# A two-layer hybrid encoder on one core: separate banks for value products, the usual weight unit last, bias lines in rounded precision, block copies in two steps, and one weight chunk of mixer B by seven products

## The chip, the cores and the metric

The kernel runs on one core of a Trainium2 chip. The time is the device time of one execution in microseconds (us), and what counts is the median of several runs; the profile is one further execution taken by the hardware profiler. Five engines work side by side: TensorE (PE in the profile; its weight loads are PEld), VectorE (DVE), ScalarE (ACT), GpSimd (POOL) and SyncE (SP, which here only issues DMAs). Each engine executes its own list of instructions strictly in order; between engines they wait on semaphores. Matmul results go to PSUM, which has eight banks of 128 partitions by 512 floats.

## The reference, cut to what matters

The input is 256 positions by 2048 features in float32. Two layers follow each other: mixer A (grouped-query attention) with a gated MLP, then mixer B (three head groups of dilated attention) with a second gated MLP, and a last RMS norm.

```python
def mixer_b(h, w_qkv, w_o, rel_bias):
    qkv = (h @ w_qkv).reshape(b, s, n_g, 3, hg, HEAD_DIM)      # 2048 -> 9216
    for g, (window, dil) in enumerate(B_GROUPS):               # (128,1),(512,4),(2048,16)
        o, lz = dilated_group(qkv[:, :, g, 0], qkv[:, :, g, 1], qkv[:, :, g, 2],
                              rel_bias[:, g * hg:(g + 1) * hg], window, dil)
    wts = jax.nn.softmax(jnp.stack(log_zs, axis=0), axis=0)
    y = jnp.concatenate([wts[g][..., None] * outs[g] for g in range(n_g)], axis=2)
    return y.reshape(b, s, B_WIDTH) @ w_o

def conv_ffn(h, w_up, conv_w, conv_b, w_down):
    u = depthwise_conv(h @ w_up, conv_w) + conv_b              # 2048 -> 11264, 3 taps over positions
    gate, val = jnp.split(u, 2, axis=-1)
    return (jax.nn.silu(gate) * val) @ w_down                  # 5632 -> 2048
```

## The kernel before

**Products.** All large products are of 256 positions (two halves `m`, 128 each) by weights that stream in from memory. A weight tile is 512 rows by 512 columns, called a chunk `kg` of an output block `n`; it is loaded in two raw buffers of 512 KB (`raw`, `NRAW = 6` of them). Precision near float32 is kept by splitting both operands into a rounded high part and the rest: ACT writes `wh` (L128), DVE writes `wl = raw - wh` (L129), and PE does three products, `xh*wh`, `xh*wl`, `xl*wh` (L153 to L155). One raw buffer makes twelve matmuls of 512 columns, here called a usual unit, or `c`. The split pairs `wh`/`wl` lie in a ring of `NHL = 3`; the down projection of the MLP adds a fourth. `split_raw` gives these instructions a priority 45 places ahead, so they stand early in their engines' lists. `feed` and `project` run over the chunks; accumulators are bank pairs 0/1 and 2/3 in turn (`new_acc`), banks 4 to 7 go round for everything else (`ps_tile`).

**Seven products.** In the down projection two of the chunks are done for two output blocks `n0`, `n1` together by Strassen's scheme with seven products in place of eight (`project_pair`, L215). The two weight blocks are cut into "11", "12", "21", "22"; DVE adds blocks in place (L242), each product `P` takes six matmuls, and sums of the inputs (`forms`) are made beforehand. Products 2, 3 and 4 go straight into C11, C12 and C21; products 1, 5, 6 and 7 have banks of their own (M1, M5, M6, M7) and are added to the result by `combine`. Usual units of the other chunks stand between the products (`weave`).

**Woven work.** Attention and activation work is written as generators; `step()` advances the oldest one after each unit, so its instructions stand between matmuls. `heads_T_dve` turns a key or query tile into head-major form: DVE transposes 32x32 blocks into a staging tile (L335), then sixteen block copies place them, twelve on ACT (L347) and four on POOL (L345), all in one step (`turned`, L351). The staging tile is one buffer (tag `vl` in mixer B). `late_transpose` does the same for the next stage's input; its last block goes by PE.

**Mixer B** (L917): for each half `hf` of the heads and each group `g`: key projection, query projection, then three value projections. `k_gen` and `s_gen` scale (L686), turn, form logits (L305, or L307 to L309), add bias, and take exponentials (L986). `v_gen` turns probabilities and multiplies by values; for `g == 0` the products of heads 0 and 1 share one bank, as do those of 2 and 3 (L1037).

**Bias lines** (L892) makes the position bias during the first MLP: a one-hot table times the bias table, six float32 matmuls (L908), written to memory and read back in skewed form.

## Time and profile before

| what | value |
|---|---|
| median of 3 runs | 2263.91 us (2262.77 to 2263.95) |
| the profiled execution | 2264.28 us, of which span 2262.5 us |
| matmuls | 10093 records, 2241.2 us busy |
| VectorE, ScalarE, GpSimd busy | 1671.3, 1535.6, 299.2 us |
| read from memory | 429.20 MB, 192 GB/s over the span |

The span is the time between the first and the last instruction of the profile; the rest of the execution's time lies around it. The page of the profile has the busy time of each engine, the chain of work that ended last, the costliest groups of instructions and the DMA issues. Further views are asked of the trace: which engine waited for which, the instructions in order of time (start, length, engine, line, output and inputs; idle time ahead of them and who ended it stand in brackets), groups of equal instructions in a stretch, and busy times by stretch. Matmuls overlap, so a record of 0.39 us does not mean that each takes that long on the engine: the distance between two starts does.

### The profile page before, as it was taken

The page shows a single profiled execution, that of the slowest core. Times are in us where ns is not written, and L with a number is a line of the kernel's source. Part 1 is how long each engine was busy: PE and PEld are TensorE (multiplying, and loading weights), DVE is VectorE, ACT ScalarE, POOL GpSimd, SP SyncE. Part 2 cuts the span into 40 slices and gives each one's busy share as a digit, 9 for nine tenths or more (in the row PEclk, how much of TensorE's full clock was granted, in tenths as well). Part 3 has the DMA queues.
Part 4 walks back from the last instruction along what each step waited for, and adds up shares of the span by engine and source line. Part 5 has one row for each costly group of instructions (what it writes and reads, how often), then busy time and mean ns, then how long its engine had stood idle before and what let it go on. Part 6 is the DMA issues. An engine that isn't in the chain of part 4 may idle for free.

```text
span 2262.5 us, 28925 instructions
## 1 busy us (share of the span) xinstructions
PE 2241.2 (99%) x10093; PEld 1853.5 (82%) x10093; DVE 1671.3 (74%) x2267; ACT 1535.6 (68%) x2400; POOL 299.2 (13%) x436
## 2 busy tenths in 40 slices
PE   9999999999999999999999999999999999999998
PEld 7788888888888888888878887888888888888886
DVE  6776678888878788856575557465888788688895
ACT  6665777777547777767775777565777754577763
POOL 2211102210001010121130103000101100001101
PEclk9999999999999999999999999999999999999999
DMA  8444667765665655666655564655665656556654
GB/s 297 158 149 149 191 198 217 227 198 192 207 203 187 199 190 188 204 223 203 190 173 180 177 194 160 186 195 188 197 191 192 204 188 212 188 193 193 226 191 136
DMA packets 126452, 437.43 MB, mean 193 GB/s; under 512 B 17265, under 2 KB 18033, under 8 KB 126305
## 3 DMA queue, kind: packets, MB, share of 16 engines
q1 hardware_dynamic: 119744, 425.64, 58.3%
q0 software_dynamic: 6128, 9.38, 1.7%
q8 instruction: 79, 1.29, 0.2%
q14 instruction: 69, 0.56, 0.1%
q10 hardware_dynamic: 432, 0.56, 0.1%
HBM read 429.20 MB, written 6.29 MB: 192 GB/s over the span
## 4 chain that ended last, share of the span: by engine, by line
PE 91%; DVE 3%; ACT 2%; issue 1%; DMA 1%; POOL 1%; SPq 0%; POOLq 0%; DVEq 0%; ACTq 0%
PE acc L154 25%; PE acc L155 25%; PE acc L153 25%; PE acc L273 5%; PE acc L275 5%; PE acc L278 5%; DVE wl L129 1%; ACT tM L347 1%; ACT wh L128 1%; PE ps L305 1%; PE ps L307 0%; PE ps L309 0%; POOL pp L345 0%; PE ps L308 0%; DMA raw<-in_w_down_dram 0%
## 5 line engine op out<-in xcount | busy, mean ns | idle before, releaser
L129 DVE TENSOR_TENSOR wl<-raw,wh 128x1024 fp32r<-128x1024 f32 x828 | 1019.0, 1237 | 437.8 <-ACT wh L128 435.2
L128 ACT ACTIVATE wh<-raw 128x1024 fp32r<-128x1024 f32 x828 | 872.6, 1058 | 499.9 <-PE acc L155 307.0
L153 PE MATMUL acc<-wh,xh 128*128 128x512 f32 x2176 | 851.2, 392 | 0.6 <-ACT wh L164 0.6
L154 PE MATMUL acc<-wl,xh 128*128 128x512 f32 x2176 | 848.2, 390 | 1.6 <-DVE wl L129 1.4
L155 PE MATMUL acc<-wh,xh 128*128 128x512 f32 x2176 | 847.7, 390 | 0.0
L154 PEld LDWEIGHTS acc<-wl,xh 128*128 128x128 f32 x2176 | 408.8, 188 | 88.6 <-DVE wl L129 4.4
L155 PEld LDWEIGHTS acc<-wh,xh 128*128 128x128 f32 x2176 | 408.6, 188 | 84.7
L153 PEld LDWEIGHTS acc<-wh,xh 128*128 128x128 f32 x2176 | 408.9, 188 | 84.0 <-ACT wh L164 1.0
L345 POOL COPY u<-t 32x256 f32<-32x256 f32 x176 | 110.6, 628 | 1027.1 <-DVE t L455 1018.9
L273 PE MATMUL acc<-wh,ah 128*128 128x512 f32 x520 | 202.5, 389 | 1.5 <-DVE h L408 1.5
L275 PE MATMUL acc<-wh,al 128*128 128x512 f32 x520 | 202.3, 389 | 0.0
L154 PE MATMUL acc<-wl,ah 128*128 128x512 f32 x480 | 187.1, 390 | 1.0 <-DVE wl L129 1.0
L153 PE MATMUL acc<-wh,ah 128*128 128x512 f32 x480 | 187.2, 390 | 0.3 <-DVE cu L628 0.3
L155 PE MATMUL acc<-wh,al 128*128 128x512 f32 x480 | 186.8, 390 | 0.0
L347 ACT ACTIVATE u<-t 32x256 f32<-32x256 f32 x352 | 147.7, 420 | 13.9 <-DVE t L455 6.0
L278 PE MATMUL acc<-wl,ah 128*128 128x512 f32 x520 | 146.1, 389 | 0.0
L273 PEld LDWEIGHTS acc<-wh,ah 128*128 128x128 f32 x520 | 97.6, 188 | 22.6 <-DVE h L408 2.3
L278 PEld LDWEIGHTS acc<-wl,ah 128*128 128x128 f32 x520 | 97.6, 188 | 20.3
L275 PEld LDWEIGHTS acc<-wh,al 128*128 128x128 f32 x520 | 97.6, 188 | 20.2
L154 PEld LDWEIGHTS acc<-wl,ah 128*128 128x128 f32 x480 | 90.2, 188 | 20.0 <-DVE wl L129 1.8
L153 PEld LDWEIGHTS acc<-wh,ah 128*128 128x128 f32 x480 | 90.1, 188 | 19.1 <-DVE cu L628 0.9
L155 PEld LDWEIGHTS acc<-wh,al 128*128 128x128 f32 x480 | 90.1, 188 | 18.6
(182 smaller groups left out, 1729.0 us busy)
## 6 DMA issues: line engine op xcount, KB each, us to landing
raw<-in_w_up_dram SPq DMA_DIRECT2D x352, 512.0 KB, 4.4
raw<-in_w_down_dram SPq DMA_DIRECT2D x176, 512.0 KB, 4.8
raw<-in_w_b_dram SPq DMA_DIRECT2D x144, 512.0 KB, 4.4
raw<-in_w_bo_dram SPq DMA_DIRECT2D x48, 512.0 KB, 3.9
raw<-in_w_a_dram SPq DMA_DIRECT2D x40, 512.0 KB, 4.5
raw<-in_w_ao_dram SPq DMA_DIRECT2D x32, 512.0 KB, 4.0
raw<-in_w_a_dram SPq DMA_DIRECT2D x16, 256.0 KB, 6.6
h<-in_x_dram SPq DMA_DIRECT2D x4, 512.0 KB, 8.4
```

Of the source, the lines that this page charges most:

```text
L128: nc.scalar.activation(wh, r, AF.Copy)
L129: nc.vector.tensor_tensor(wl, r, wh.bitcast(F32), ALU.subtract)
L153: nc.tensor.matmul(accs[m], xh, wh[:, j, :], start=st, stop=False)
L154: nc.tensor.matmul(accs[m], xh, wl[:, j, :], start=False, stop=False)
L155: nc.tensor.matmul(accs[m], xl, wh[:, j, :], start=False, stop=sp)
L273: nc.tensor.matmul(acc[k], xh, wh[:, j, :], start=k in fresh, stop=False)
L275: nc.tensor.matmul(acc[k], xl, wh[:, j, :], start=False, stop=False)
L278: nc.tensor.matmul(acc[k], xh, wl[:, j, :], start=False, stop=last[k] == i and j == 1)
L305: nc.tensor.matmul(o, lh[ls], rh[rs], start=start, stop=stop)
L345: nc.gpsimd.tensor_copy(dst, src)
L347: nc.scalar.activation(dst, src, AF.Copy)
```

## The change

Five things are changed.

1. In `v_gen` every product of group 0 takes its own bank.
2. In the first down pair of each MLP's first half, the first and the eighth product are no longer followed by a usual unit, so that two usual units move behind the last products; and `combine` takes M7 where it took M5 in its last sum, which is algebraically equal.
3. The bias table is split into a rounded high part and the rest, which stand in the two halves of the partitions, against a one-hot table that is loaded twice; the matmul is then one rounded product.
4. `turned` copies its sixteen blocks in two steps of eight, with one idle step fewer behind it.
5. In mixer B the key and query projections of groups 1 and 2, in both halves, are made together by `seven`: chunk 3 by seven products, chunks 0 to 2 by twelve usual units. The input forms are made once, at the end of the first MLP (`last_forms`). M1, M5, M6 and M7 take banks from the common four and are moved out at once (`product_done`).

```diff
+    def project_pair(w, n0, n1, lhs, forms, units, late, early_done, n0_done, product_done=None):
+        if product_done:
+            acc = dict(zip(("C11", "C21", "C12", "C22"), new_acc() + new_acc()))
...
+            for k, *_ in todo:
+                if k not in acc:
+                    acc[k] = ps_tile()
...
+            if product_done and kind == "P" and home[p][0] == "M":
+                product_done(home[p], acc.pop(home[p]))
             if i == last_s:
                 early_done(acc)
-            if i == last["C21"]:
+            if i == max(last["C11"], last["C21"]):
                 n0_done(acc)
-            step()
+            if not product_done or kind == "c" or p in (1, 5, 7, 4):
+                step()
...
     def turned(o, s, pool, tag):
         t = turn_blocks(s, pool, tag)
+        for part in (range(8), range(8, 16)):
+            yield
+            place_blocks(o.rearrange("p j (m t) -> p j m t", m=2), t, "paaa", part)
+
+    def last_forms(hT, turn_pair, n, g):
+        fm = hT["forms"] = {f: new_hT(4 * n + i)[:2] for i, f in enumerate((1, 0, 2, 4))}
...
+        c0 = scaled(0)
+        put(1, c0[:, :, :P])
+        put(0, c0[:, :, P:])
         yield
-        place_blocks(o.rearrange("p j (m t) -> p j m t", m=2), t, "paaa")
+        c1 = scaled(1)
+        put(2, c1[:, :, :P])
+        put(4, c1[:, :, P:])
+        x0, s1, s2, s3, s4 = (tmp(k) for k in (12, 13, 14, 15, 20))
+        yield
+        nc.scalar.activation(x0, c0[:, :, P:], AF.Copy)
+        nc.vector.tensor_tensor(s3, c0[:, :, :P], x0, ALU.subtract)
+        nc.vector.tensor_tensor(s1, c1[:, :, P:], x0, ALU.subtract)
+        put(7, s3)
+        put(5, s1)
+        yield
+        nc.vector.scalar_tensor_tensor(s2, s1, -1.0, c0[:, :, :P], ALU.mult, ALU.subtract)
+        nc.vector.tensor_tensor(s4, c1[:, :, :P], s2, ALU.add)
+        put(6, s2)
+        put(3, s4)
...
+                    lone = (ps[0], ps[7]) if lead > 1 and hf == 0 else ()
                     for u in ps:
-                        units += [u] + [c.pop(0) for _ in range(min(1, len(c)))]
+                        units += [u] + [c.pop(0) for _ in range(min(1, len(c))) if u not in lone]
...
-                    nc.vector.tensor_tensor(u, acc["M5"], u, ALU.add)
-                    nc.vector.tensor_tensor(hcol(1, n1), hcol(1, n1), u, ALU.subtract)
+                    nc.vector.tensor_tensor(v, acc["M7"], v, ALU.add)
+                    nc.vector.tensor_tensor(hcol(1, n1), hcol(1, n1), v, ALU.subtract)
...
-            oh = wp.tile([P, 1024], F32, tag="wh9", name="oh")
-            nc.gpsimd.dma_start(oh, onehot)
+            of = lp.tile([P, 2, 512], F32, tag="tT", name="of").rearrange("p a c -> p (a c)")
+            oh = wp.tile([P, 1024], F32R, tag="wh9", name="oh")
...
+            nc.scalar.activation(oh, of, AF.Copy)
+            nc.vector.tensor_copy(rs, rb)
+            nc.vector.tensor_tensor(rs[64:], rb[64:], rs[64:].bitcast(F32), ALU.subtract)
+            nc.vector.tensor_copy(lh, rs.bitcast(F32)[:, :, None].to_broadcast([P, 24, 32]))
...
                     def value(i):
-                        j = i % 2
+                        j = 0 if g == 0 else i % 2
...
+                def seven(n0, n1, sums, n0_ready, n1_ready):
+                    (k0, k1), (q0, q1) = sums
+
+                    def product_done(k, t):
+                        if k != "M6":
+                            nc.scalar.activation({"M1": k0, "M5": q1, "M7": k1}[k], t, AF.Copy)
+                            return
+                        nc.vector.tensor_tensor(q0, t, k0, ALU.add)
+                        nc.vector.tensor_tensor(k1, k1, q0, ALU.add)
+                        nc.vector.tensor_tensor(q0, q0, q1, ALU.add)
+                        nc.vector.tensor_tensor(q1, k1, q1, ALU.add)
+
+                    def n0_done(a):
+                        nc.vector.tensor_tensor(k0, a["C11"], k0, ALU.add)
+                        nc.vector.tensor_tensor(k1, a["C21"], k1, ALU.add)
+                        n0_ready([k0, k1])
+
+                    cs = [("c", k, i) for i2 in range(2) for k in kgs[:3] for i in (2 * i2, 2 * i2 + 1)]
+                    units = [cs.pop(0)]
+                    for p, c in zip(ORDER, (1, 2, 1, 2, 1, 1, 3)):
+                        units += [("P", 3, p)] + [cs.pop(0) for _ in range(c)]
+                    a = project_pair(w_b, n0, n1, hT, {3: hT["forms"]}, units, None, lambda a: None,
+                                     n0_done, product_done)
+                    nc.vector.tensor_tensor(q0, a["C12"], q0, ALU.subtract)
+                    nc.vector.tensor_tensor(q1, a["C22"], q1, ALU.subtract)
+                    n1_ready([q0, q1])
+
                 for g in range(3):
                     bts = biases(hf, g)
+                    n0, n1 = 6 * g + 2 + hf, 6 * g + hf
+                    if g == 0:
+                        start(k_gen(g, project(w_b, n0, hT, kgs)))
+                        start(s_gen(g, project(w_b, n1, hT, kgs), bts))
+                    else:
+                        sums = [[bp.tile([P, 512], F32, tag=t, name=nm("ms"), bufs=2) for _ in range(2)]
+                                for t in ("pTh", "pTl")]
+                        seven(n0, n1, sums, lambda a: start(k_gen(g, a)), lambda a: start(s_gen(g, a, bts)))
```

The order of the units in a pair is thus c P1 c P2 cc P5 c P3 cc P7 c P6 c P4 ccc: the first six usual units belong to the key block (C11, C21), the last six to the query block (C12, C22). The keys are complete when P4 is done, three units ahead of the queries.

Three places show how instructions now stand. The first is VectorE at the turning of a key tile in mixer B, before (`wl` is the low part of a weight unit, `stg` the scaled keys, `tT` the staging tile, `lg` the logits of the group before):

```order
L129 TENSOR_TENSOR wl_9481<-raw_9476,wh_9480 128x1024 [waits DMAHW1_49,Activation_49]
L335 STREAM_TRANSPOSE tT_9473<-stg_9418 128x512 [waits Activation_49] x2
L975 SCALAR_TENSOR_TENSOR lg_9450<-ps_9443,bt_8852 128x512 [waits PE_49]
L129 TENSOR_TENSOR wl_9513<-raw_9477,wh_9512 128x1024 [waits DMAHW2_49,Activation_49]
L977 TENSOR_REDUCE nmx_8855<-lg_9450 128x2 [waits DVE_49]
L129 TENSOR_TENSOR wl_9533<-raw_9528,wh_9532 128x1024 [waits DMAHW3_49,Activation_49]
```

The query tile's turning stood a whole projection later in the list.

The second is VectorE from the end of one key and query pair into the next, now (`ms_9243`, `ms_9244` are the key sums, `ms_9245`, `ms_9246` the query sums, `tT_9609` the keys' staging tile, `tT_9711` the queries', which is the same buffer):

```order
L129 TENSOR_TENSOR wl_9641<-raw_9638,wh_9640 128x1024 [waits DMAHW6_49,PE_49,Activation_49]
L1151 TENSOR_TENSOR ms_9244<-acc_9248,ms_9244 128x512 [waits DVE_49]
L129 TENSOR_TENSOR wl_9681<-raw_9678,wh_9680 128x1024 [waits DMAHW7_49,PE_49,Activation_49]
L344 STREAM_TRANSPOSE tT_9609<-stg_9587 128x512 [waits Activation_49]
L129 TENSOR_TENSOR wl_9699<-raw_9696,wh_9698 128x1024 [waits DMAHW0_49,PE_49,Activation_49]
L1160 TENSOR_TENSOR ms_9245<-acc_9249,ms_9245 128x512 [waits PE_49]
L1161 TENSOR_TENSOR ms_9246<-acc_9250,ms_9246 128x512 [waits PE_49]
L129 TENSOR_TENSOR wl_9717<-raw_9714,wh_9716 128x1024 [waits DMAHW1_49,DVE_49,Activation_49]
L245 TENSOR_TENSOR raw_9696<-raw_9696,raw_9780 128x1024 [waits DMAHW5_49,DVE_49]
L344 STREAM_TRANSPOSE tT_9711<-stg_9666 128x512 [waits Activation_49,Pool_49]
L344 STREAM_TRANSPOSE tT_9711<-stg_9666 128x512 [waits Activation_49]
L129 TENSOR_TENSOR wl_9743<-raw_9740,wh_9742 128x1024 [waits DMAHW2_49,PE_49,Activation_49]
```

The queries' transposes now stand seven rows behind the keys' and ahead of the split of unit P2 of the next pair (`wl_9743`); the split of P1 is `wl_9699`, that of the second usual unit `wl_9717`.

The third is ScalarE over the same stretch, now (`wh` is the high part of a weight unit, `kT` the turned keys):

```order
L356 ACTIVATE kT_9608<-tT_9609 32x8x32 [waits DVE_49]
L356 ACTIVATE kT_9608<-tT_9609 32x8x32 x5
L128 ACTIVATE wh_9716<-raw_9714 128x1024 [waits DMAHW1_49,PE_49,Activation_49]
L356 ACTIVATE kT_9608<-tT_9609 32x8x32 x6
L747 ACTIVATE stg_9666<-ms_9245,rstd_8855 128x512 [waits DVE_49]
L747 ACTIVATE stg_9666<-ms_9246,rstd_8855 128x512 [waits DVE_49]
L128 ACTIVATE wh_9742<-raw_9740 128x1024 [waits DMAHW2_49,PE_49,Activation_49]
```

The twelve copies of the keys, the two scalings of the queries and three weight splits form one chain here; in the kernel before, the twelve copies stood in runs of seven, three and two between weight splits, and the queries' scalings a projection later.

More of the change, by code (lines that the diff above doesn't have):

```diff
@@ L213, in project2 @@
         return a1
-    def project_pair(w, n0, n1, lhs, forms, units, late, early_done, n0_done):
+    def project_pair(w, n0, n1, lhs, forms, units, late, early_done, n0_done, product_done=None):
         home = {1: "M1", 2: "C11", 3: "C12", 4: "C21", 5: "M5", 6: "M6", 7: "M7"}
-        place = ("M1", "M5", "M6", "M7", "C11", "C21", "C12", "C22")
-        b = bank_at[0]
-        acc = {k: bank((4, 5, 6, 7, 2 - b, 3 - b, b, b + 1)[i], "acc") for i, k in enumerate(place)}
+        if product_done:
+            acc = dict(zip(("C11", "C21", "C12", "C22"), new_acc() + new_acc()))
+        else:
+            place = ("M1", "M5", "M6", "M7", "C11", "C21", "C12", "C22")
+            b = bank_at[0]
+            acc = {k: bank((4, 5, 6, 7, 2 - b, 3 - b, b, b + 1)[i], "acc") for i, k in enumerate(place)}
         def touched(u):
@@ L366, in late_transpose @@
             yield
-            yield
             for j in range(4):
@@ L373, in late_transpose, with turn_pair @@
         yield
-        for kp in range(2):
-            if kp:
-                yield
+        def turn_pair(kp):
             t = ps_tile()
@@ L382, in late_transpose @@
                                         h[:, m, kt * P:(kt + 1) * P], ident)
+            return t
+        if g == 2:
+            yield from last_forms(hT, turn_pair, n, g)
+            return
+        for kp in range(2):
+            if kp:
+                yield
+            t = turn_pair(kp)
             for j in range(2):
@@ L711, in heads_T_dve @@
         yield from turned(dst, s, pool, tag)
-        yield
         yield
```

43 lines of the change are left out of this document (33 added, 10 removed).

## The prediction, made before the changed kernel was run

> **What bounds the kernel now.** I read the page's busy times first, then TensorE's waits, then the stretches that the change touches.
>
> ```profile
> PE 2241.2 (99%) x10093; PEld 1853.5 (82%) x10093; DVE 1671.3 (74%) x2267; ACT 1535.6 (68%) x2400; POOL 299.2 (13%) x436
> PE 91%; DVE 3%; ACT 2%; issue 1%; DMA 1%; POOL 1%; SPq 0%; POOLq 0%; DVEq 0%; ACTq 0%
> ...
> PE ps L307 <- DVE al L291: 4.5, 2, 2.3
> PE acc L154 <- DVE wl L129: 2.4, 5, 0.7
> PE acc L273 <- DVE h L408: 1.5, 2, 1.0
> PE ps L396 <- DVE warm L393: 1.5, 1, 1.5
> ```
>
> TensorE is busy 99% of the span and is 91% of the chain of waits; it stands idle only 2262.5 - 2241.2 = 21 us, most of it at the start and the end. The last four rows are its waits (in all, times, longest). So there are two ways to be faster: fewer matmul passes, or these waits; and one way to be slower: new waits, since VectorE and ScalarE feed it. What a matmul costs and how full the feeders are is read from stretches (stretch, length, then busy time and records of PE, PEld, DVE, ACT, POOL):
>
> ```profile
> 700.00:850.00 150.00, 150.00 (x664) 124.20 (x663) 123.16 (x190) 114.19 (x182) 18.11 (x28) 1.00 0.61 194
> 1053.00:1097.00 44.00, 44.00 (x203) 36.66 (x202) 25.37 (x28) 31.78 (x60) 8.12 (x12) 1.00 0.66 212
> 877.00:928.00 51.00, 51.00 (x227) 42.23 (x226) 47.20 (x55) 34.62 (x47) 2.58 (x4) 1.00 0.55 183
> ```
>
> The first lies in an up projection, with nothing but 512-column matmuls: 150.00/663 = 0.226 us each. The second is a key and a query projection in mixer B: VectorE 58%, ScalarE 72%. The third is a down pair that already does seven products for eight: VectorE 93%, ScalarE 68%, and TensorE without a gap.
>
> **The change part by part.** *Fewer matmuls.* Each of four pairs saves one of eight products, six matmuls: 24 x 0.226 = **5.4 us**.
>
> *Bias lines.* A wide one, then a narrow one:
>
> ```profile
> 363.74 1.02 PE L908 MATMUL ps<-oh,lh 128*128 128x512 f32 x2
> 364.19 0.80 PE L153 MATMUL acc<-wh,xh 128*128 128x512 f32 x1
> 364.83 0.40 PE L154 MATMUL acc<-wl,xh 128*128 128x512 f32 x1
> ...
> 398.19 0.59 PE L908 MATMUL ps<-oh,lh 128*128 128x256 f32 x2
> 398.43 0.59 PE L153 MATMUL acc<-wh,xh 128*128 128x512 f32 x1
> 398.86 0.40 PE L154 MATMUL acc<-wl,xh 128*128 128x512 f32 x1
> ```
>
> From the line's start to the second matmul behind it is 1.09 and 0.67 us; less 0.23 for the one between, a line costs 0.86 and 0.44. A rounded pass is 0.23, and 0.12 for 256 columns (1162.77 to 1162.88 below). Saved: 2 x 0.63 + 4 x 0.32 = **2.6 us**.
>
> *Value products.*
>
> ```profile
> 1159.12 1.68 DVE L291 TENSOR_TENSOR pTl<-pp,pTh 128x512 fp32r<-128x512 f32 x2
> 1162.77 0.28 PE L307 MATMUL ps<-pTh,vh 128*128 128x256 f32 x1
> 1162.88 0.28 PE L308 MATMUL ps<-pTl,vh 128*128 128x256 f32 x1
> 1164.97 1.23 DVE L129 TENSOR_TENSOR wl<-raw,wh 128x1024 fp32r<-128x1024 f32 x1 [0.21 <-ACT wh L128]
> 1168.16 0.42 DVE L291 TENSOR_TENSOR al<-ps,ah 128x256 fp32r<-128x256 f32 x1
> 1168.63 0.39 PE L307 MATMUL ps<-pTh,vh 128*128 128x256 f32 x1 [2.26 <-DVE al L291]
> ```
>
> The second product waits until the first has been read from the bank they share. Its own inputs (`pTl`, both at 1159.12) are long there, and the next unit's split (1164.97) ends at 1166.2, when TensorE could go on. In its own bank the product does not wait: **4.5 us** for the two halves, bounds 0 and 4.5; I take all of it, since both other inputs are on time.
>
> *The usual unit last.* `L273 <- DVE h L408` is the first unit of the second down pair, waiting for the key bank's residual. With a unit of 12 x 0.226 = 2.7 us behind the last product, two residual sums of 0.69 fit even between splits: **1.5 us**, bounds 0 and 1.5. The changed last sum of `combine` is the same count and costs nothing: in that stretch `h` is not waited for.
>
> *Copies in two steps.*
>
> ```profile
> 949.20 5.11 ACT L347 ACTIVATE tM<-tT 32x256 f32<-32x256 f32 x12
> 954.33 2.01 ACT L128 ACTIVATE wh<-raw 128x1024 fp32r<-128x1024 f32 x2
> 955.43 2.36 DVE L129 TENSOR_TENSOR wl<-raw,wh 128x1024 fp32r<-128x1024 f32 x2 [4.48 <-ACT wh L128]
> 956.71 0.50 PE L154 MATMUL acc<-wl,ah 128*128 128x512 f32 x1 [0.49 <-DVE wl L129]
> ```
>
> Twelve copies in a row hold back a weight split, VectorE waits 4.48 us and TensorE 0.49. Two runs of six leave room for a split. Of the five waits of `L154` (2.4 us) I take the two of this kind, **1.0 us**; bounds 0 and 2.4.
>
> *Forms at the end of the first MLP.* ScalarE gets nine and VectorE eight more instructions of 256 columns:
>
> ```profile
> L128 ACT ACTIVATE wh<-raw 128x1024 fp32r<-128x1024 f32 x6 | 6.4, 1061 | 8.0 <-PE acc L155 8.0
> L294 ACT ACTIVATE xh<-ps,gain 128x256 fp32r<-128x256 f32 x4 | 1.9, 466 | 2.7 <-DVE xh L297 2.7
> L297 DVE SCALAR_TENSOR_TENSOR xh<-ps,gain,xh 128x256 fp32r<-128x256 f32 x4 | 1.9, 481 | 1.1 <-ACT xh L294 1.1
> ```
>
> That is 9 x 0.47 = 4.2 and 8 x 0.48 = 3.8 us. In 980 to 1000 us, where these groups lie, ScalarE waited 8.0 us for TensorE; the first forms are needed four units (11 us) after their transposes. Nothing on the path; 4.2 us if that cover were gone. The table's rounding (one copy) and the second table load lie in the MLP, where ScalarE is free a third of the time: nothing.
>
> *The load of a pair.* What is added, from groups of the stretch 1053 to 1097 (first three rows) and of the down pair (last two):
>
> ```profile
> L129 DVE TENSOR_TENSOR wl<-raw,wh 128x1024 fp32r<-128x1024 f32 x16 | 19.5, 1222 | 15.9 <-ACT wh L128 15.9
> L347 ACT ACTIVATE kT<-tT 32x256 f32<-32x256 f32 x12 | 5.0, 415 | 0.2
> L686 ACT ACTIVATE stg<-acc,rstd 128x512 f32<-128x512 f32 x5 | 3.3, 679 | 1.2 <-PE acc L155 1.2
> ...
> L242 DVE TENSOR_TENSOR raw<-raw,raw 128x1024 f32<-128x1024 f32 x8 | 9.8, 1223 | 0.9 <-DMA raw<-in_w_down_dram 0.9
> L408 DVE TENSOR_TENSOR h<-acc,h 128x512 f32<-128x512 f32 x1 | 0.7, 685 | 0.0
> ```
>
> Splits go from 16 to 19; VectorE adds 3 x 1.22 + 4 block sums x 1.22 + 8 sums x 0.69 = 14.0 us, ScalarE 3 x 1.06 + 3 bank copies x 0.68 = 5.2. VectorE then has 39.4 us and ScalarE 37.0 us in 42.6: 92% and 87%. That is less than the time, so on average they keep up, as in the down pair; but here ScalarE is fuller and the ring has three splits, not four.
>
> *The joint behind a pair* is where it is tightest. Let T be the end of the pair on TensorE. ScalarE's list there is six key copies (2.5 us), a split, six copies, two query scalings, the split of P2. The query sums (two of 0.69) wait for T, but the copies and the split ahead of the scalings end later. If the first six copies are done at T, the scalings end at T + 1.06 + 2.5 + 1.36 = T + 4.9, the two transposes (0.70 each) at T + 6.3, the split of P2 at T + 7.5. TensorE wants it at T + 2.7 + 1.4 + 2.7 + 0.9 = T + 7.7. So the margin is 0.2. The key tile, however, is turned only when VectorE has done, from P6's end at T - 12.2 on, five key and product sums (3.4), the M6 sum (0.7), four splits (4.9) and two transposes (1.4): T - 1.8 at the earliest, and the six copies end at T + 0.7. TensorE then waits 0.5. With VectorE a split and a half behind, which its lead of 1 to 3 us allows, it waits up to 3.4. I take 1.2. Behind the second pair of a half come usual units; their split is wanted at T + 8.4, so the wait is 0 to 2.7; I take 0.8. Queued behind the late transposes are all later weight splits, so nothing else absorbs it. Two halves: 2 x 2.0 = **4.0 us lost**, bounds 0 and 12.2. I stay near the lower end because the down pair, equally full, shows none.
>
> The sum: -5.4 - 2.6 - 4.5 - 1.5 - 1.0 + 4.0 = -11.0 us. The profiled execution took 2264.28, so 2253.3; the median of the runs is 0.4 below it: **2253 us**.
>
> **The rivals.** *The joints wait in full.* VectorE and ScalarE hand each other work (logits, maximum, exponential) in these stretches, so both may stand behind: 12.2 lost, 2261. For it: 92% and 87%; against: the down pair.
>
> *The value products find a new wait* in place of the old: VectorE's list there is packed, and the value unit behind needs its split. Then 4.5 is not gained: 2257.4. Against it: the rows above.
>
> *The ring of raw buffers decides; slower.* From P5 to P4 the four blocks hold four of six raw buffers, and usual units share two. A buffer is busy for the landing, 1.06 and 1.22 us; a usual unit comes every 4.1 us, so landings up to 2 x 4.1 - 2.3 = 5.9 us are hidden.
>
> ```profile
> raw<-in_w_b_dram SPq DMA_DIRECT2D x144, 512.0 KB, 4.4
> h<-in_x_dram SPq DMA_DIRECT2D x4, 512.0 KB, 8.4
> ```
>
> The median is 4.4 us; at 8.4, the longest of that size, each of five units would be (10.7/2) - 4.1 = 1.25 us late, 25 us over four pairs: 2278. Beyond some 7 us of landing the change loses. Against it: the down pair has the same ring and waited 0.9 us for loads, on VectorE only.
>
> *GpSimd's copies become long.* Four of a tile's sixteen copies are its own, and the queries' transposes wait for them (one staging buffer).
>
> ```profile
> L345 POOL COPY kT<-tT 32x256 f32<-32x256 f32 x8 | 5.1, 632 | 43.0 <-DVE tT L335 22.1 <-PE ps L305 20.7
> L345 POOL COPY tM<-tT x12: 393/804/2397, 938.5 to 966.3; 32x256 f32<-32x256 f32 x12
> ```
>
> Beside an idle VectorE a copy takes 0.63 us; where splits stand back to back (938 to 966, shortest, median, longest) up to 2.4. Four of those end at T + 7.7, the split of P2 at T + 10.3: 2.6 and 1.9 late at the two joints, 9.0 in all instead of 4.0, so 2258. [...]
>
> **How the numbers follow.** The forecast has 0.66, joints in full 0.10, value wait 0.11, raw ring 0.07, GpSimd 0.06. The forecast's own range is 2247 (all gains, no loss at the joints: 2264.3 - 15.0 - 0.4 = 2248.9, and 1.4 more of `L154`'s waits) to 2257. With the first three rivals that are not slower it reaches 2262, so the range is **2247 to 2262**; the raw ring and tails are left out. What a measurement can tell from no change is 0.2%, 4.5 us, so "same" is 2259.4 to 2268.4. Faster: 0.66 + 0.11 + 0.06, less 0.03 for the forecast's upper tail = 0.80; same: 0.10 + 0.03 = 0.13; slower 0.07.
>
> **What would show it.** Right: 24 matmul records fewer of 512 columns, and six fewer bias records; no `ps <- DVE al` among TensorE's waits; no wait at the second down pair; four waits of 0 to 3 us on `wl` or `wh`, 40 to 45 us apart, in the second and third product stage of each half. Wrong: waits on `raw` by VectorE of over 2 us in the pairs (raw ring), GpSimd copies with a mean above 1 us there, a wait for `pTl` or `wl` at the value products, or TensorE waits in the pairs away from the joints.

## The result and the profile after

| | before | changed kernel |
|---|---|---|
| median of 9 runs each | 2263.91 us | 2258.31 us (2255.28 to 2260.76) |
| ratio to before, 95% interval | | 0.9976 (0.9965 to 0.9986) |
| profiled execution, span | 2264.28, 2262.5 us | 2258.32, 2256.5 us |

The change made the kernel 5.6 us faster, about half of the 10.9 us that were forecast. The page of the changed kernel first: busy times, then the chain of work that ended last.

```profile
PE 2234.5 (99%) x10063; PEld 1847.3 (82%) x10063; DVE 1722.9 (76%) x2337; ACT 1555.4 (69%) x2434; POOL 305.0 (14%) x438
PE 91%; ACT 3%; issue 2%; DVE 2%; DMA 1%; POOL 1%; SPq 0%; POOLq 0%; DVEq 0%; ACTq 0%
```

TensorE has 30 records fewer, 24 matmuls of the products and 6 of the bias lines. Its waits (in all, times, longest):

```profile
PE acc L154 <- DVE wl L129: 4.0, 7, 0.9
PE acc L279 <- ACT wh L128: 3.6, 3, 1.8
PE ps L314 <- issue: 1.0, 1, 1.0
```

`ps <- DVE al` and `h L408` are gone. New are waits on ScalarE's high part (`wh`) at the seven products (L279), and one at the logits (L314). Stretches show where the time went. First the two pairs and the first value projection, then the two other value projections, for each half of the heads; before, then after (columns as in the prediction's second fence):

```profile
1028.30:1143.20 114.90, 114.90 (x534) 96.05 (x532) 66.34 (x73) 85.05 (x154) 16.43 (x25) 1.00 0.62 196
1143.20:1194.40 51.20, 48.89 (x235) 40.47 (x234) 40.06 (x79) 37.69 (x71) 21.42 (x33) 1.00 0.53 172
1240.60:1355.50 114.90, 114.90 (x534) 96.02 (x532) 66.71 (x73) 83.64 (x153) 12.57 (x20) 1.00 0.59 185
1355.50:1406.70 51.20, 48.87 (x235) 40.45 (x234) 39.84 (x78) 37.67 (x71) 20.86 (x32) 1.00 0.51 167
```

```profile
1024.60:1142.50 117.90, 115.35 (x521) 94.32 (x520) 91.34 (x103) 93.12 (x166) 19.03 (x25) 0.99 0.58 191
1142.50:1190.90 48.40, 48.40 (x235) 40.63 (x234) 39.78 (x78) 37.45 (x71) 22.33 (x33) 1.00 0.57 181
1237.10:1353.70 116.60, 113.34 (x520) 93.38 (x520) 91.24 (x103) 92.00 (x165) 15.26 (x20) 1.00 0.56 181
1353.70:1402.10 48.40, 48.40 (x236) 40.67 (x234) 39.80 (x78) 37.51 (x71) 21.58 (x32) 1.00 0.54 175
```

The value projections gain 2 x (51.20 - 48.40) = 5.6 us. The stretches with the pairs grow, by 3.0 and 1.7 us, though each has twelve matmuls (2.7 us) fewer: 4.7 + 5.4 = 10.1 us are lost there. The value projection at the end of such a stretch has the same matmuls in both kernels. In the first half of the heads, before and then after:

```profile
1120.10:1143.20 23.10, 23.10 (x110) 19.31 (x108) 12.62 (x15) 16.79 (x32) 2.53 (x4) 1.00 0.59 189
1118.40:1142.50 24.10, 23.60 (x109) 19.09 (x108) 13.79 (x17) 20.66 (x41) 3.55 (x7) 1.00 0.59 193
```

So 1.0 us is lost there, behind the second pair, and 0.8 in the second half of the heads (23.90 against 23.10). The other 8.3 us, 4.7 and 3.6, are lost in the pairs, most of it behind the first pair of each half. ScalarE's list behind the first pair, whose end T on TensorE is 1070.22 (start, length, engine, line, output and inputs; idle time ahead in brackets):

```profile
1064.38 0.72 ACT L747 ACTIVATE stg<-ms,rstd 128x512 f32<-128x512 f32 x1 [1.55 <-DVE ms L1150]
1065.01 1.99 ACT L128 ACTIVATE wh<-raw 128x1024 fp32r<-128x1024 f32 x2
1069.04 0.73 ACT L747 ACTIVATE stg<-ms,rstd 128x512 f32<-128x512 f32 x1 [2.04 <-DVE ms L1151]
1069.67 1.05 ACT L128 ACTIVATE wh<-raw 128x1024 fp32r<-128x1024 f32 x1
1070.80 2.56 ACT L356 ACTIVATE kT<-tT 32x256 f32<-32x256 f32 x6
1073.38 1.06 ACT L128 ACTIVATE wh<-raw 128x1024 fp32r<-128x1024 f32 x1
1074.46 2.54 ACT L356 ACTIVATE kT<-tT 32x256 f32<-32x256 f32 x6
1077.03 1.33 ACT L747 ACTIVATE stg<-ms,rstd 128x512 f32<-128x512 f32 x2
1078.27 1.99 ACT L128 ACTIVATE wh<-raw 128x1024 fp32r<-128x1024 f32 x2
```

ScalarE waits 1.55 and 2.04 us for VectorE's key sums, and from 1069.04 on it never stops. VectorE's list up to then, from the last logits sum and maximum of the group before (L1048, L1050) over the M6 sum (L1144) and the key's last sum (L1151) to the key tile's second transpose (L344), has no gap over 0.4 us:

```profile
1058.39 0.68 DVE L1048 SCALAR_TENSOR_TENSOR lg<-ps,bt 128x512 f32<-128x512 f32 x1
1059.11 0.69 DVE L1050 TENSOR_REDUCE nmx<-lg 128x2 f32<-128x512 f32 x1
1059.72 1.22 DVE L129 TENSOR_TENSOR wl<-raw,wh 128x1024 fp32r<-128x1024 f32 x1
1060.85 0.68 DVE L1144 TENSOR_TENSOR ms<-ps,ms 128x512 f32<-128x512 f32 x1
...
1068.32 0.69 DVE L1151 TENSOR_TENSOR ms<-acc,ms 128x512 f32<-128x512 f32 x1
1068.92 1.22 DVE L129 TENSOR_TENSOR wl<-raw,wh 128x1024 fp32r<-128x1024 f32 x1
1070.05 0.71 DVE L344 STREAM_TRANSPOSE tT<-stg 128x512 f32<-128x512 f32 x1
```

The first six copies end at T + 3.1, where the prediction had T + 0.7 at the earliest. The split of P2, the first of the last two of `wh`, ends at 1079.31. TensorE in order of time:

```profile
1079.36 0.70 PE L279 MATMUL acc<-wh,xh 128*128 128x512 f32 x1 [1.84 <-ACT wh L128]
1079.87 0.63 PE L281 MATMUL acc<-wh,xh 128*128 128x512 f32 x1
1080.29 0.63 PE L279 MATMUL acc<-wh,xh 128*128 128x512 f32 x1
```

It starts P2 2.0 us late (by the distance between two starts, less the usual one; the bracket counts idle time alone), and then each matmul starts 0.43 us after the one before instead of 0.23. The stretches say why (the third value from the end is the granted clock):

```profile
1076.08:1079.49 3.41, 1.57 (x8) 0.97 (x7) 2.20 (x4) 3.36 (x7) 0.27 (x1) 1.00 0.47 154
1079.49:1082.90 3.41, 3.41 (x9) 2.61 (x10) 3.14 (x3) 3.32 (x6) 3.28 (x4) 0.50 0.00 0
1082.90:1086.32 3.42, 3.42 (x16) 2.80 (x15) 2.26 (x3) 3.32 (x7) 0.88 (x1) 1.00 0.77 232
```

Behind the wait the clock stood at half for 3.41 us, which cost eight matmuls 0.2 us each, 1.6 us more. In the second half of the heads the same wait is 1.75 us and the clock stays, but the logits come 1.1 us late.

A second loss lies in the first MLP. VectorE, before and after, where it waits for the bias table (`rb`):

```profile
279.31 0.56 DVE L902 COPY lh<-rb 128x768 f32<-128x768 f32 x1 [4.06 <-DMA rb<-in_rel_bias_dram]
```

```profile
280.51 0.18 DVE L968 CAST rs<-rb 128x24 fp32r<-128x24 f32 x1 [4.82 <-DMA rb<-in_rel_bias_dram]
280.61 1.23 DVE L129 TENSOR_TENSOR wl<-raw,wh 128x1024 fp32r<-128x1024 f32 x1
```

The table is loaded twice, behind two loads of the one-hot table, and the last one lands 1.2 us later than the only one did before. The weight split queued behind it ends at 281.84 us, 0.4 us later than before, and the unit that wants it comes 0.6 us earlier in this profile, so TensorE stands idle for 0.8 us at 281.1, where it did not wait before. From one matmul near 260 us to another near 300 us it takes 40.95 us, against 39.95 between the same two before: 1.0 us is lost.

### The profile page after: what moved, and what is told of

Its sections match the earlier page's. It is cut to its first block, busy times and chain, and to the rows that moved or that the text cites. A ratio compares the mean times of both kernels' runs of the same rounds, so it can differ in the third digit from the quotient of the medians.

```text
span 2256.5 us, 29002 instructions
## 1 busy us (share of the span) xinstructions
PE 2234.5 (99%) x10063; PEld 1847.3 (82%) x10063; DVE 1722.9 (76%) x2337; ACT 1555.4 (69%) x2434; POOL 305.0 (14%) x438
## 4 chain that ended last, share of the span: by engine, by line
PE 91%; ACT 3%; issue 2%; DVE 2%; DMA 1%; POOL 1%; SPq 0%; POOLq 0%; DVEq 0%; ACTq 0%
PE acc L154 22%; PE acc L155 22%; PE acc L153 22%; PE acc L279 7%; PE acc L281 7%; PE acc L284 7%; DVE wl L129 1%; ACT wh L128 1%; ACT kT L356 1%; PE ps L314 1%; PE ps L318 1%; PE ps L317 1%; PE ps L316 0%; PE ps L928 0%; ACT tM L356 0%
## 5 line engine op out<-in xcount | busy, mean ns | idle before, releaser
L129 DVE TENSOR_TENSOR wl<-raw,wh 128x1024 fp32r<-128x1024 f32 x840 | 1032.5, 1237 | 386.4 <-ACT wh L128 383.4
L128 ACT ACTIVATE wh<-raw 128x1024 fp32r<-128x1024 f32 x840 | 883.3, 1057 | 473.7 <-PE acc L155 272.2
L154 PE MATMUL acc<-wl,xh 128*128 128x512 f32 x1920 | 748.7, 390 | 4.4 <-DVE wl L129 3.5
L153 PE MATMUL acc<-wh,xh 128*128 128x512 f32 x1920 | 748.9, 390 | 0.6 <-ACT wh L164 0.6
L155 PE MATMUL acc<-wh,xh 128*128 128x512 f32 x1920 | 748.1, 390 | 0.0
L154 PEld LDWEIGHTS acc<-wl,xh 128*128 128x128 f32 x1920 | 360.5, 188 | 81.9 <-DVE wl L129 7.3
L155 PEld LDWEIGHTS acc<-wh,xh 128*128 128x128 f32 x1920 | 360.5, 188 | 74.6
L153 PEld LDWEIGHTS acc<-wh,xh 128*128 128x128 f32 x1920 | 360.4, 188 | 74.4 <-ACT wh L164 1.3
L279 PE MATMUL acc<-wh,ah 128*128 128x512 f32 x520 | 202.3, 389 | 0.0
L279 PEld LDWEIGHTS acc<-wh,ah 128*128 128x128 f32 x520 | 97.6, 188 | 20.3
```

Source lines behind the costliest of these rows:

```text
L128: nc.scalar.activation(wh, r, AF.Copy)
L129: nc.vector.tensor_tensor(wl, r, wh.bitcast(F32), ALU.subtract)
L153: nc.tensor.matmul(accs[m], xh, wh[:, j, :], start=st, stop=False)
L154: nc.tensor.matmul(accs[m], xh, wl[:, j, :], start=False, stop=False)
L155: nc.tensor.matmul(accs[m], xl, wh[:, j, :], start=False, stop=sp)
L279: nc.tensor.matmul(acc[k], xh, wh[:, j, :], start=k in fresh, stop=False)
```

## The experiments

All ratios are to the kernel before, with 95% intervals.

**1. Without the pairs.**

```diff
-                    if g == 0:
+                    if g < 3:
                         start(k_gen(g, project(w_b, n0, hT, kgs)))
```

> Changes 1 to 4 alone: the key and query projections of groups 1 and 2 are done by usual units again (the input forms are still made). Theory A (the four pairs lose some 10 us at their joints, against 5.4 us of fewer matmuls): 2258.3 - 10.0 + 5.4 = 2253.7 us. Rival B (the joints lose the 4.0 us of the prediction, and the shortfall lies in the other four edits): 2258.3 - 4.0 + 5.4 = 2259.7 us.

Measured: 2255.25 us, 0.9964 (0.9952 to 0.9977). The pairs cost 3.1 us net, so with the 5.4 of their matmuls 8.5 us are lost: nearer to theory A than to B, a little less than A said. The two intervals overlap, so the size is loose. TensorE's waits:

```profile
PE acc L154 <- DVE wl L129: 4.2, 5, 1.8
```

The waits on L279 and L314 are gone. The longest of the rest is at 283 us, behind the bias table, which here came in at 281.74; the clock fell there too:

```profile
280.64:284.05 3.41, 1.59 (x7) 1.00 (x7) 2.24 (x5) 1.39 (x3) 0.00 (x0) 1.00 0.01 2
284.05:287.46 3.41, 3.41 (x10) 2.66 (x9) 2.98 (x4) 1.82 (x2) 0.00 (x0) 0.50 0.58 166
```

From the same matmul near 260 us to the same near 300 us this profile takes 43.40 us, 3.4 more than before. So rival B has a part in it after all, and the fifth experiment takes it up.

**2. Without the block sums in mixer B.**

```diff
-                with tc.high_priority(offset=AHEAD):
-                    nc.vector.tensor_tensor(dst, dst, src, ALU.add)
+                if not product_done:
+                    with tc.high_priority(offset=AHEAD):
+                        nc.vector.tensor_tensor(dst, dst, src, ALU.add)
```

> The in-place sums of weight blocks of the four pairs in mixer B are left out (16 instructions of 1.22 us on VectorE), so the key and query values are not the reference's. Theory A1 (ScalarE's chain at the joint starts late because VectorE, with no idle time from 1059 to 1073 us, makes the key sums late): ScalarE's idle times of 1.55 and 2.04 us ahead of the two key scalings shrink to under 0.8 in all, TensorE's waits at the joints fall from 2.0 and 1.75 us to under 0.7, the clock stays at 1.00, about 2250 us. Rival A2 (ScalarE's own list at the joint, twelve copies, two scalings and the splits, is too long even when VectorE is on time): the waits stay above 1.2 us and the time within 1.5 us of 2258.3.

Measured: 2254.78 us, 0.9961 (0.9947 to 0.9975). The second pair now begins at 1072.51; ScalarE ahead of it:

```profile
1063.76 0.73 ACT L748 ACTIVATE stg<-ms,rstd 128x512 f32<-128x512 f32 x1 [0.37 <-DVE ms L1151]
1068.42 0.72 ACT L748 ACTIVATE stg<-ms,rstd 128x512 f32<-128x512 f32 x1 [0.95 <-DVE ms L1152]
1070.22 2.56 ACT L357 ACTIVATE kT<-tT 32x256 f32<-32x256 f32 x6
```

The key copies begin 2.3 us ahead of the pair's end instead of 0.6 behind it, and the waits at the first product fall to nothing and 0.3 us. The two idle times are 1.3 us in all, not under 0.8. VectorE has done the last logits maximum of the group before at 1058.9, ahead of P6's end, and makes the M6 sum at 1060.50, 12.0 us ahead of the pair's end instead of 9.4. So VectorE's load is what starts ScalarE late (A1). The gain is less than expected; in this profile the logits wait 1.2 and 1.1 us in the two halves, as they did once in the changed kernel, and the bias table's wait costs 3.6 us instead of 1.0.

**3. Eight of sixteen copies on GpSimd**, for the key and query tiles of groups 1 and 2.

```diff
-            place_blocks(o.rearrange("p j (m t) -> p j m t", m=2), t, "paaa", part)
+            place_blocks(o.rearrange("p j (m t) -> p j m t", m=2), t, places, part)
...
-                    yield from heads_T_dve(kT, ks, bp, "vl")
+                    yield from heads_T_dve(kT, ks, bp, "vl", "papa" if g else "paaa")
...
-                    yield from heads_T_dve(qT, qs, bp, "vl")
+                    yield from heads_T_dve(qT, qs, bp, "vl", "papa" if g else "paaa")
```

> Of the sixteen block copies of each key and query tile of groups 1 and 2, eight instead of four go to GpSimd: ScalarE's chain at the joint loses 4 x 0.42 = 1.7 us. Theory A: the wait at the second pair's first product falls from 2.0 and 1.75 us to about 0.3 and with it the slow clock behind it; 2 x 3.5 us, so about 2251 us. Rival C (GpSimd takes over as the bound, eight copies of 0.65 us or more beside a full VectorE, and the query's transposes wait for its last one): waits as before or longer, 2258 us or more.

Measured: 2251.99 us, 0.9949 (0.9937 to 0.9962): theory A. In 1020 to 1145 us TensorE has one wait, on a low part:

```profile
PE acc L284 <- DVE wl L129: 0.2, 1, 0.2
```

ScalarE starts as late as in the changed kernel, 0.6 us behind the pair's end. A list that is 1.7 us shorter is enough all the same.

**4. The query's scalings one step later.**

```diff
+                    if g:
+                        yield
                     qs = evac_scaled(bp, accs, rstd)
                     yield
-                    yield
+                    if not g:
+                        yield
```

> The two query scalings of groups 1 and 2 are issued one step later, so that on ScalarE the high part of the second pair's first product stands ahead of them (1.33 us less ahead of it). Theory A: the wait of 2.0 and 1.75 us falls to about 0.6, too short to slow the clock; 2 x 3 us, so about 2252 us. Rival A3 (the wait moves to the next unit, whose low part now stands behind the later transposes on VectorE): the sum of TensorE's waits in the first 20 us of the second pair stays within 0.5 us of 2.2 us and the time within 1.5 us of 2258.3.

Measured: 2259.15 us, 0.9980 (0.9971 to 0.9988). The wait at P2 fell to 0.8 us, and what it lost came back at the logits, 11 us later, with the clock at half behind it:

```profile
1089.29 1.10 PE L314 MATMUL ps<-kT,qT 128*128 128x128 f32 x4 [2.14 <-issue]
```

It moved as A3 says, only to another place: the query's twelve copies, begun later, end later. The list as a whole seems too long, rather than one piece of it badly placed.

**5. The bias table rounded on GpSimd.**

```diff
-            nc.vector.tensor_copy(rs, rb)
-            nc.vector.tensor_tensor(rs[64:], rb[64:], rs[64:].bitcast(F32), ALU.subtract)
-            nc.vector.tensor_copy(lh, rs.bitcast(F32)[:, :, None].to_broadcast([P, 24, 32]))
+            nc.gpsimd.tensor_copy(rs, rb)
+            nc.gpsimd.tensor_tensor(rs[64:], rb[64:], rs[64:].bitcast(F32), ALU.subtract)
+            nc.gpsimd.tensor_copy(lh, rs.bitcast(F32)[:, :, None].to_broadcast([P, 24, 32]))
```

> Only the rounding of the bias table (three small instructions that wait for the two late loads of the table) moves from VectorE to GpSimd, which has nothing to do there. Theory D (that wait holds back the weight split queued behind it on VectorE: TensorE lost 1.5 us near 282 us in the changed kernel's profile and 3.9 us in the profile of the first experiment, where the clock fell behind the wait): the wait on the split at 281 to 284 us is gone (under 0.3 us), and the time is 1.5 to 3.9 us less than that of the changed kernel's 2258.3, so 2254.4 to 2256.8 us. Rival E (the stall comes from the splits and input terms of that place themselves, not from the table's loads): TensorE still waits 0.8 us or more there, and the time stays within 1 us of 2258.3.

Measured: 2256.76 us, 0.9967 (0.9954 to 0.9979), 1.6 us less than the changed kernel by the medians; the intervals overlap, so the size is loose. The wait is gone: TensorE has none between 260 and 300 us. The 0.5 us that the expectation of experiment 12 puts at 281 us stand near 241 us, in every profile, that of the kernel before too. The stretch from 260 to 300 us, between the same two matmuls, bears theory D out. It takes 40.95 to 43.57 us in the seven profiles with the new table on VectorE, and 39.67 here, against 39.95 before. A row of VectorE shows another wait beside it:

```profile
281.29 0.49 DVE L306 SCALAR_TENSOR_TENSOR xh<-ps,gain,xh 128x256 fp32r<-128x256 f32 x1 [3.52 <-ACT xh L303]
```

VectorE no longer waits for the table, but for an input term that stands on ScalarE behind the rounding of the one-hot table, which waits for a load of its own. Here TensorE does not wait for it.

**6. The key's last sum earlier.** The two query sums move from the place behind M6 to the place behind the key's sums, and the second key sum stays in its PSUM bank.

```diff
-                        nc.vector.tensor_tensor(q0, q0, q1, ALU.add)
-                        nc.vector.tensor_tensor(q1, k1, q1, ALU.add)
...
-                        nc.vector.tensor_tensor(k1, a["C21"], k1, ALU.add)
-                        n0_ready([k0, k1])
+                        nc.vector.tensor_tensor(a["C21"], a["C21"], k1, ALU.add)
+                        nc.vector.tensor_tensor(q0, q0, q1, ALU.add)
+                        nc.vector.tensor_tensor(q1, k1, q1, ALU.add)
+                        n0_ready([k0, a["C21"]])
```

> The same sums in another order: the two query sums of the key and query products that VectorE makes behind M6 come behind the key's last sum, which therefore stands 1.3 to 2.5 us earlier in VectorE's list. Theory A1 (late key sums start ScalarE's chain late): ScalarE's idle time ahead of the second key scaling falls from 2.04 to under 0.8 us, TensorE's waits of 2.0 and 1.75 us at the second pair's first product to under 0.7, no slow clock there; about 2258.3 - 5 = 2253 us. Rival A2 (ScalarE's list behind the pair's end, 12 copies, 2 scalings and the splits, decides): waits above 1.2 us and the time within 1.5 us of 2258.3.

Measured: 2259.67 us, 0.9980 (0.9972 to 0.9989), a miss for A1 as it was put, and within what A2 expected. The pair ends 0.5 us later in this profile. ScalarE:

```profile
1066.66 0.69 ACT L747 ACTIVATE stg<-acc,rstd 128x512 f32<-128x512 f32 x1
1067.25 1.05 ACT L128 ACTIVATE wh<-raw 128x1024 fp32r<-128x1024 f32 x1
1070.31 1.27 ACT L356 ACTIVATE kT<-tT 32x256 f32<-32x256 f32 x3 [2.00 <-DVE tT L344]
```

The second scaling comes 2.4 us earlier and the idle time ahead of it is gone, but it stands now ahead of the copies, which wait for the tile's second transpose. VectorE makes that at 1069.57, against 1070.05: its list up to there holds the same work in another order, and there was next to no idle time in it. The wait at P2 is 2.0 us, as before.

**7. Experiments 3 and 5 together.**

> The third and the fifth experiment together: eight copies of a key or query tile on GpSimd, and the bias table rounded on GpSimd. If the two waits are independent (A and D): 2252.0 less the 2.4 us lost near 282 us in the third experiment's profile, 2249.6 us. If GpSimd's work gets in the way of itself or the gains overlap: 2251.5 us or more.

Measured: 2251.26 us, 0.9943 (0.9931 to 0.9956), between the two expectations. The second pair of the first half, in the changed kernel and here:

```profile
1070.22:1118.40 48.18, 46.32 (x203) 37.58 (x202) 39.82 (x47) 38.75 (x71) 9.11 (x11) 0.96 0.59 192
```

```profile
1070.12:1115.47 45.35, 44.95 (x203) 36.35 (x202) 39.32 (x46) 34.63 (x62) 14.53 (x18) 1.00 0.61 199
```

It is 2.8 us shorter, with the clock at full. What is left of the table's cost is a wait of 1.0 us at 284 us, on a split that stands behind the rounding of the one-hot table.

**8. Experiments 3, 5 and 6 together.**

> The third, fifth and sixth together. What is left of waits in the four pairs in the third experiment's profile is about 3 us (2.2 and 0.9); with the key's sums earlier too, A gives 1 to 2 us less than the run without it, about 2248 us. If ScalarE and GpSimd already keep up (the copies were the whole of it), the same time within 0.7 us.

Measured: 2253.78 us, 0.9951 (0.9937 to 0.9964), a miss of both: later, not earlier. Its waits name a new one that ends last:

```profile
PE ps L314 <- POOL qT L354: 2.7, 2, 1.4
```

With eight copies of the query tile, GpSimd is the last to finish ahead of the logits. In the seventh experiment it has as many; there they begin at 1077.53 us, here at 1079.91, behind a later transpose of the queries.

**9. The first edit alone**, in the kernel before.

```diff
-                        j = i % 2
+                        j = 0 if g == 0 else i % 2
```

> The kernel before, with the first edit alone: every value product of group 0 in its own bank. Theory (the two waits of 2.26 us were the whole cost and both other inputs are on time): 4.5 us less than before, so 2259.4 us against 2263.9, and no wait of TensorE on the low parts at the value products. Rival F (the edit gains more than the wait, since a wait of over 2 us also slows the clock, or brings splits forward): 6 us or more. Rival G (a new wait takes its place): 2 us or less.

Measured: 2257.89 us, 0.9973 (0.9963 to 0.9983): 6.2 us, with 3.8 to 8.4 in the interval, which holds the theory's 4.5 and rival F's 6; G is out. In its profile the two stretches of value projections are 2.8 us shorter each, 5.7 in all. A slow clock was no part of it: in the kernel before it stood at 1.00 behind the waits of 2.26 and 2.27 us.

**10. The block sums on GpSimd.**

```diff
-                    nc.vector.tensor_tensor(dst, dst, src, ALU.add)
+                    (nc.gpsimd if product_done else nc.vector).tensor_tensor(dst, dst, src, ALU.add)
```

> The sixteen in-place sums of weight blocks in mixer B go from VectorE to GpSimd; all results are kept. Theory A1 (VectorE's backlog starts ScalarE's chain late): ScalarE's idle times ahead of the two key scalings shrink from 1.55 and 2.04 us to under 1.4 in all, the waits of 2.0 and 1.75 us at the second pair's first product to under 0.5 and the slow clock goes, as in the second experiment, so 2251 to 2255 us. Rival H (GpSimd's sums are slow, 2.5 us or more each, and hold up the products that use them, or slow VectorE's instructions beside them): new waits of VectorE or ScalarE on the sums, 2258 us or more.

Measured: 2262.86 us, 0.9994 (0.9984 to 1.0003): rival H. GpSimd's groups from 1020 to 1130 us:

```profile
L245 POOL TENSOR_TENSOR raw<-raw,raw 128x1024 f32<-128x1024 f32 x8 | 23.2, 2906 | 30.8 <-DMA raw<-in_w_b_dram 24.1 <-issue 3.5 <-DVE wl L129 3.1
```

A sum takes 2.9 us instead of 1.22, and ScalarE still waits 1.55 and 2.04 us for the key sums. TensorE waits 1.4 and 2.0 us at P2, and anew for over 1 us at the logits and at the first value projection. So taking the sums off VectorE does not help when they come later than VectorE would have made them.

**11. No pairs, the table on GpSimd.**

> The first experiment (no pairs in mixer B) with the bias table rounded on GpSimd, so that edits 1 to 4 stand without the table's wait. The prediction's terms for these edits are 2.6 + 4.5 + 1.5 + 1.0 = 9.6 us; the stages of the changed kernel's trace make them 10.3. So 2253.6 to 2254.3 us against a before of 2263.9; and the pairs with shorter chains (the seventh experiment, 12.8 us below before) would then be worth 2.5 to 3.2 us of their 5.4. Rival: the table's wait was not what made the first experiment 1.5 us slower than its terms; it stays at 2255.3.

Measured: 2253.07 us, 0.9952 (0.9940 to 0.9965): 11.0 us below the kernel before, 2.2 below the first experiment. The pairs of the seventh experiment are then worth 1.8 us by the medians, less than the expected 2.5 to 3.2; the intervals overlap.

**12. The seventh, and the one-hot table rounded on GpSimd.**

```diff
-            nc.scalar.activation(oh, of, AF.Copy)
+            nc.gpsimd.tensor_copy(oh, of)
```

> The seventh experiment, and the rounding of the one-hot table (one instruction that waits for a late load on ScalarE) on GpSimd too. In the fifth experiment's profile VectorE still waited 3.5 us at 277.8 to 281.3 us for an input term that stands behind that instruction on ScalarE, and TensorE 0.5 us at 281. Theory D: that wait goes as well, 0.5 to 1.3 us less than the seventh experiment, so 2250.0 to 2250.8 us, and no wait of TensorE over 0.2 us between 270 and 300 us. Rival: the input terms are late for reasons of their own, no difference (2251.3 us).

Measured: 2249.57 us, 0.9938 (0.9924 to 0.9951), the best of all: 14.2 us below the kernel before and 8.7 below the changed one. TensorE has no wait between 260 and 300 us, where the seventh and the eleventh had one of 1.0 and 0.8: theory D in the trace. Its interval overlaps that of the seventh, and the fifth had no wait there either, so how much this step gives is open.

## Why the prediction was right or wrong

| term | predicted | measured, us |
|---|---|---|
| 24 matmuls | -5.4 | 24 records fewer, -5.4 |
| bias lines, their passes | -2.6 | -2.7 (between the same matmuls, 355 to 460 us) |
| bias table's loads and rounding | 0 | +1.0 (this trace; up to +3.6 in others), +1.6 and +2.2 (experiments 5, 11) |
| value products | -4.5 | -5.6 (stretches), -6.2 (experiment 9) |
| second down pairs' waits | -1.5 | -2.1 (0.8 and 1.3, between the same matmuls) |
| copies in two steps | -1.0 | -0.8: the wait at 956.71 us is gone, that at 242 stays |
| joints behind first pairs | +2.4 | +8.3 (stretches) |
| joints behind second pairs | +1.6 | +1.8 (stretches) |
| joints in all | +4.0 | +10.1 (stretches), +8.5 (experiment 1), +9.1 (11 against 5) |

The terms by the changed kernel's trace add up to -5.5 us; its span is 6.0 shorter.

*The direction and the kinds of gain and loss held.* The gains came as said or a little better, but for the copies. (The bias lines' sum, 2 x 0.63 + 4 x 0.32, is 2.5 and not 2.6.) Experiment 11, which is these terms without the pairs, is 11.0 us below before, where the prediction's 9.6 stand.

*The step that failed is the joint behind the first pair*, "I take 1.2", chosen "near the lower end because the down pair, equally full, shows none": 4.7 and 3.6 us were lost there. The mechanism is the one described: ScalarE's copies, scalings and split behind VectorE's key sums. Three things made it three to four times as large. The key tile was turned at T + 0.5, not T - 1.8, because VectorE ran 2.8 us behind when it began the chain (the M6 sum at T - 9.4, not T - 12.2). The chain that the prediction counts from P6's end, T - 12.2 or 1058.0 us, leaves out what stood ahead of the M6 sum then: the rest of a split, the last logits sum and maximum of the group before, and a fifth split. The prediction had the case of a late VectorE, "a split and a half behind", with up to 3.4 us, and did not take it; a split and a half is only 1.8 us, and the 3.4 needs some 2.9, close to what was measured. The wait of 2.0 us halved the clock for one stretch, 1.6 us more, which no row of before shows. And the query's copies, which the prediction's chain ends ahead of, made the logits late by 1.1 us in the second half. The down pair was the wrong comparison: it has nothing that is scaled, turned and copied behind it, so a full VectorE there delays no such chain of ScalarE's. That is argued from the lists; no run tests it.

Behind the second pairs the size, 0.8, was about right, but by luck: the waits that came, 0.7 us on `wl` at 1133.2 and 1344.4 us, lie 15 us behind the pair's end, at a split that stands behind the query's copies on ScalarE, and not at T + 8.4.

Experiments 2 and 3 cut the chain at either end, VectorE's load or ScalarE's copies, and either removes the wait at P2. Experiments 4, 6 and 10 move pieces of it about, and gain nothing.

*The second failed step is small:* "the table's rounding (one copy) and the second table load lie in the MLP, where ScalarE is free a third of the time: nothing". The cost is no busy time. It is an instruction that waits for a slow load, at the head of VectorE's list. The time from issue to landing was in reach: 5.1 us in the profile of the kernel before, where VectorE waited 4.06 us for it. In the changed kernel it is 5.6 us, the median of two.

*The rivals.* The joints in full (12.2 us lost) came nearest. The value products found no wait of 2 us, only 0.7 at a split in the first value projection, counted with the joints. The raw ring did not decide; VectorE's waits for loads in the first half's pairs (1024 to 1118 us of the changed kernel) are one:

```profile
DVE raw L245 <- DMA raw<-in_w_b_dram: 1.2, 1, 1.2
```

GpSimd's copies did become longer at the second pair, for the query tile above all, with a mean above the 1 us that the prediction gave as a sign (groups from 1070 to 1118 us):

```profile
L354 POOL COPY qT<-tT 32x256 f32<-32x256 f32 x4 | 4.4, 1108 | 5.8 <-DVE tT L344 5.7
L354 POOL COPY kT<-tT 32x256 f32<-32x256 f32 x6 | 4.2, 702 | 21.2 <-DVE tT L344 21.1
```

In the kernel before, the mean of 0.63 us that the prediction sets beside an idle VectorE is that of six key copies of 0.39 to 0.40 us and two of 1.30 and 1.40, which had a split of VectorE beside them for over 1 us each. The copies at the second pair did not set the end there: they ended at 1083.8 us, ScalarE's copies of the same tile at 1089.2. Experiment 8 shows where they do.

What stays open: VectorE's delay at the joint was narrowed to the logits work and the fifth split, which come on time without the block sums (experiment 2), but no run moves the logits work alone; and the sizes of the joints by the trace and by the medians differ by 1 to 1.6 us. The table's wait, which differs from profile to profile, is in these medians too.

## What to carry to other kernels

When work is added to engines that feed a full TensorE, look for the chain that starts when a stage ends (sums, scaling, turning, copying) and cost it from where the feeder really stands, not from its mean load; if it crosses two engines, shorten the chain by giving part of it to an idle third one: by the medians that took 6.3 us off the changed kernel (experiment 3, where GpSimd had been busy 14%), while reordering only moved the wait (0.8 and 1.4 us more in experiments 4 and 6). An added instruction that waits for a load holds back what stands behind it on that engine: in the changed kernel VectorE waited 4.82 us for the bias table, and 1.0 us was lost there; in experiment 5, with the rounding on GpSimd, TensorE did not wait. So put it on an engine with nothing behind it. And keep single waits of TensorE under some 2 us: the one of 2.0 us in the changed kernel, which fell into one cell of the grid described below, cost 1.6 us more.

## What the hardware showed that was not expected

Records of the granted clock change on a grid of 3.413 us in every trace: in the changed kernel the slow one, 1079.49 to 1082.90 us, is one cell long, and the full ones ahead of it and behind it are 315 and 342. With TensorE's idle time summed in each cell of that grid (distances between starts, less the usual one), all fourteen traces agree, the start and the end of the program left aside:

| idle in one cell of 3.413 us | cells | clock in the next cell |
|---|---|---|
| 2.00, 2.05, 2.09, 2.12, 2.17, 2.27, 2.27, 2.31 | changed kernel, experiments 1, 2, 4, 5, 6 | 0.5, each time, for one cell |
| 1.94 (before), 1.91, 1.90, 1.83 and less | the others | 1.00 |

A longer wait that fell across the edge of two cells did not slow the clock: the one of 2.42 us in the kernel before left 1.94 in one cell and 0.48 in the next, and the clock stayed at 1.00. So 2.00 us idle in one cell were enough in these traces, and 1.94 were not.
